# Hybrid RG-LRU and attention encoder block: four weight sums of group H on VectorE instead of in the transfers, and turned gate rows turned and stored at other ticks

## The chip, the cores and the metric

The kernel runs on one core of a Trainium2 chip. The time is device time in microseconds (us) of one execution. The kernel before takes 885.68 us, the median of three runs (883.79 to 886.96).

A core has five engines that run side by side, each with its own queue of instructions, worked off in order: TensorE (PE in the profile, with its weight loads as PEld), VectorE (DVE), ScalarE (ACT), GpSimd (POOL) and SyncE (SP). SP, POOL and ACT also issue transfers (DMA) between DRAM and the on-chip memory. A transfer can add what it brings to what already stands in the destination; here only POOL issues such transfers.

## The reference, cut to what matters

One layer, 256 tokens, width 2048, all in float32:

```python
xn = rms_norm(x, norm_pre_w)
u_lru, g_lru, q, k, v, g_attn, m_lru, m_attn = split(xn @ w_in)      # w_in is 2048 x 13312
h   = rg_lru forward + rg_lru backward of a width-4 convolution of u_lru
y_a = h * silu(g_lru)
y_b = windowed_gqa(rope(q), rope(k), v, sink) * silu(g_attn)
merged = sigmoid(m_lru) * (y_a @ w_proj_a) + sigmoid(m_attn) * (y_b @ w_proj_b)
out = x + rms_norm(merged @ w_out, norm_post_w)
```

The change is in how half of `g_attn` is made: columns 1024 to 2047 of that gate, which the kernel calls group H.

## The kernel before, in words

All the weights stream from DRAM through one list of steps (`START`, `MERGE`, `OUT`), some 190 of them, each with 128 x 2048 float32 numbers (1 MB) of weights in two halves. To keep float32 accuracy, every half `raw` is split in two: ScalarE casts it to a short form `wh` (L222), VectorE subtracts that from the original and gets the remainder `wl` (L224). TensorE then makes three products per block: `wh` with the two parts of the activations, and `wl` with the first part. So each step costs ScalarE two casts and VectorE two subtractions of 128x1024.

Six stretches of columns are not multiplied plainly but by a seven-product scheme (class `Seven`, groups L, H, M, N, A, O; the matmuls are on L435). Four quarter blocks of the weights, (0,0), (0,1), (1,0) and (1,1), make seven products m1 to m7, taken in the order m1, m2, m5, m3, m6, m7, m4. The weights of the products m1, m5, m6 and m4 are running sums in a cell `x`: it is loaded with quarter (0,0), then (0,1), (1,1) and (1,0) are added in turn. The cell `y` is loaded with (1,1) for m3, and (0,1) is added for m7. Each cell exists for two inner halves (0, 1) with two tiles each (a, b): `Hx0a`, `Hx0b`, `Hx1a`, `Hx1b`, and `Hy..` likewise. The first load of a cell is a plain transfer by SP (L197); each addition is an adding transfer by POOL (L195), 512 KB per tile. For the groups named in the table `ADDED`, some of these additions are made otherwise: m6 needs the quarter (1,1) that m3 has just put in `y`, so VectorE adds `y` to `x` (L227), right behind the subtraction that makes m3's `wl`. Before the change this is so for A, O and N.

An adding transfer must wait until the subtraction L224 of the step before has read the cell, and the cast of its own step must wait until it has landed.

The products of H give rows of tokens, where attention needs rows of channels. `silu_rows` handles the four results, named `hr200`, `hr210`, `hr211` and `hr201` in order of time: a VectorE combination (L797), a sigmoid (L824), a product (L825), then four transposes on TensorE into a PSUM bank pair `ht` (L831), a ScalarE copy out of it (L832) and a store of 256 KB to DRAM by SP (L839, `parksga<-hr`), from where the gate is fetched much later.

When all this stands in the queues is set at the build. Time is counted in ticks, one for a product step and two for a plain block. `at(tick, fn)` and `soon(fn, d)` put the instructions of `fn` into the queues when the list reaches that tick. `seconds` holds the ticks at which the second block of a pair begins; a turn is put at the first of them that lies more than two ticks ahead, since it takes one of the two PSUM pairs that plain blocks also use. The store is put five ticks behind the turn.

Almost all large tiles (`wh`, `wl`, the cells, `hr`, gates, parked rows) come from one pool of 45 buffers. Which buffer a new tile gets is decided at the build from the order in which old tiles are given up. A tile's first writer then waits for the last readers of the old one, and where the last reader is a store, for its landing. The raw weights have a ring of three buffers of their own, so SP's queue is in step with VectorE: a load of raw weights (L210) waits for the subtraction that frees its buffer, and what stands behind it in SP's queue waits too.

Of the kernel before, what the change touches and what calls it, by code (L numbers as in the profile page):

```python
# [64 lines left out]
LRU = (-4, 0, 0, 0, 0, 0, 0, 0)  # L65
QUADS = {"u": ("w_in", U0), "v": ("w_in", V0), "p": ("w_proj_a", 0),
         "b": ("w_proj_b", 0), "o": ("w_out", 0)}
ADDED = {'A': {'m3': 'm6', 'm2': 'm4'}, 'O': {'m3': 'm6'}, 'N': {'m3': 'm6'}}
PAIRS = {"g": GL0, "h": GA0, "w": U0, "k": K0, "q": Q0}
SEVENS = {"L": ("w_in", ML0 + 1024), "M": ("w_in", ML0), "N": ("w_in", MA0), "A": ("w_in", MA0 + 1536), "H": ("w_in", GA0 + 1024), "O": ("w_out", 0)}  # L70

# [39 lines left out]
def body(ctx, tc, x, x0, xT, wall, wlru, pvec, npost, ident_d, mask_d, rope_d, out):  # L111
# [9 lines left out]
    def unit(name, dt=F32, shape=(P, 4, S)):  # L121
        return units.tile(list(shape), dt, tag="u", name=name)
# [4 lines left out]
    def banks(name, shape=(P, 2, 2, S)):  # L127
        return psum.tile(list(shape), F32, tag="mm", name=name, bufs=2)

    def half_unit(name, tag, dt=F32, bufs=2):  # L130
        return small.tile([P, 2, S], dt, tag=tag, name=name, bufs=bufs)
# [20 lines left out]
    now = [0]  # L152

    def ticks(i=None):
        return sum(1 if p[0] == "part" else 2 for p in plan[:len(steps) if i is None else i])

    def at(hs, fn):
        assert hs >= now[0], (hs, now[0])
        due.setdefault(hs, []).append(fn)
# [9 lines left out]
    seconds, hs, n = [], 0, 0  # L169
# [7 lines left out]
    def soon(fn, d=1):  # L177
        at(now[0] + d, fn)
# [11 lines left out]
    def load(cell, p, add=False):  # L190

        w = wall[row[content(p)]]
        for h in range(2):
            if add:
                nc.gpsimd.dma_start(flat(cell[h]), w[:, h * 1024:(h + 1) * 1024], accum_op=ALU.add)  # L195
            else:
                nc.sync.dma_start(flat(cell[h]), w[:, h * 1024:(h + 1) * 1024])  # L197
# [14 lines left out]
    def split(q, c=0, w=1024, cast=nc.scalar.copy, only=None):  # L212
# [10 lines left out]
        if only != "h":  # L223
            nc.vector.tensor_tensor(ls, raw, hs.bitcast(F32), ALU.subtract)  # L224
            if plan[i][0] == "part" and plan[i][2] in ADDED.get(plan[i][1], ()):
                x = flat(groups[plan[i][1]].cells["x", plan[i][3]][h])
# [137 lines left out]
    def x_sum(name, s, q):  # L364
        t = unit(name, F32R, (P, 4, 2, P))
        nc.sync.dma_start(t.rearrange("p a b c -> p a (b c)").bitcast(F32), away[q][:, SUMS.index(s)])
        return t

    class Seven:
# [22 lines left out]
        def fetch(self, p, lead):  # L392
            m, q = p[2:]
            fresh = ("m1", "m3") if self.sums is None else ()
            if self.sums is None:
                if lead == 4 and m in fresh:
                    self.start(self.where(m), q)
                if lead == 4 and SEVEN[m][0][0] == "s" and self.name in "NA":
                    self.kept[m, q] = x_sum(f"{self.name}{m}{q}", SEVEN[m][0], q)
            if lead == 5 and m in ("m5", "m6", "m7", "m4")[self.sums is not None:] and m not in ADDED.get(self.name, {}).values():  # L400
                load(self.cell(m, q), p, True)
# [394 lines left out]
    def combine(to, ps, other, sign):  # L796
        nc.vector.scalar_tensor_tensor(to, ps, float(sign), other, ALU.mult, ALU.add if sign > 0 else ALU.subtract)  # L797
# [17 lines left out]
    def silu_rows(g):  # L815

        def done(t, c, ps, other, sign):
            u = unit(f"hr{g}{c}{t}")
            f, y = flat(u)[:, 0:512], u[:, 2:4].rearrange("p a (b s) -> p (a b) s", b=2)
            rt = rtok[:, t:t + 1]  # L820

            def sigmoid(src):
                sg = flat(half_unit(f"hs{c}{t}", "p"))
                nc.scalar.activation(sg, src, AF.Sigmoid, scale=rt)  # L824
                soon(lambda: nc.vector.scalar_tensor_tensor(f, src, rt, sg, ALU.mult, ALU.mult))  # L825
                at(min(b for b in seconds if b > now[0] + 2), turn)

            def turn():
                pt = banks(f"ht{c}{t}", (P, 4, P))
                for j in range(4):  # L830
                    nc.tensor.transpose(pt[:, j], f[:, j * P:(j + 1) * P], ident)  # L831
                nc.scalar.copy(y, pt)  # L832
                soon(store, 5)

            def store():
                key = "sga", g + c
                if key not in parked:
                    parked[key] = dram.tile([P, 1024], F32, name=f"parksga{g + c}")
                nc.sync.dma_start(parked[key].rearrange("p (j s) -> p j s", j=4)[:, :, t * P:(t + 1) * P], y)  # L839

            if other is None:
                sigmoid(ps)
            else:
                combine(f, ps, other, sign)
                soon(lambda: sigmoid(f))
        return done
# [317 lines left out]
    b, n = ticks(), ticks(len(plan))  # L1164
# [159 lines left out]
```

## Time and profile before

| | |
|---|---|
| median of three runs | 885.68 us (883.79 to 886.96) |
| the profiled execution's own time | 884.68 us |
| its span (first to last instruction) | 882.9 us |
| TensorE busy | 862.4 us |
| VectorE busy | 750.3 us |
| ScalarE busy | 657.3 us |
| transfers, mean over the span | 277 GB/s |
| the stretch of group H | 248 to 357 us |

The profile shows one execution. Times in its rows are us from the span's start; a row of the time line has start, duration, engine, line, operation, output<-inputs, shapes, count, and in square brackets how long the engine had stood idle before it and what ended that. A row of the waits has the sum, the count and the longest. Names stand without buffer numbers there: `wl` is any remainder tile, `hr` any of the four gate rows. TensorE is busy nearly all the time, so what counts is what makes it stand still, and not how busy the others are on average.

### The profile page before, as it was taken

The numbers are of one execution on the slowest core, as the hardware profiler recorded it, in microseconds if no ns is written. First come the engines' busy times: TensorE is split into PE (matmuls) and PEld (weight loads), VectorE is DVE, ScalarE is ACT, GpSimd is POOL, SyncE is SP. The second block draws the span as 40 slices with busy tenths as digits, with TensorE's granted clock in tenths as the row PEclk, the third lists the DMA queues.
The fourth block names the chain that finished last, engine by engine and source line by source line (L and its number), as shares of the span: only waits on it lengthen the run. The fifth ranks groups of instructions, "written<-read, shape, count | busy, mean of one in ns | idle before, by whom it ended". The sixth has DMA issues, their size and how long they took to land.

```text
span 882.9 us, 12249 instructions
## 1 busy us (share of the span) xinstructions
PE 862.4 (98%) x4378; PEld 733.9 (83%) x4378; DVE 750.3 (85%) x999; ACT 657.3 (74%) x939; POOL 73.0 (8%) x105
## 2 busy tenths in 40 slices
PE   9999999999999979999999999999999999999996
PEld 8888888888888868788888888778888888788885
DVE  6998999898898869797897887897669778998886
ACT  7689698969879868987976779996558545665654
POOL 0000001022011200112100020000000100000200
PEclk9999999999999999999999999999999999999999
DMA  9757699999999985999989998798999987988982
GB/s 328 275 191 250 196 315 290 278 298 250 306 255 350 260 206 195 293 270 295 280 270 328 305 288 301 251 324 334 272 327 370 298 325 215 309 311 316 266 205 95
DMA packets 68045, 244.77 MB, mean 277 GB/s; under 512 B 6416, under 2 KB 24592, under 8 KB 53264
## 3 DMA queue, kind: packets, MB, share of 16 engines
q1 hardware_dynamic: 52480, 198.37, 61.4%
q0 software_dynamic: 11520, 41.95, 25.1%
q10 hardware_dynamic: 3984, 3.67, 1.3%
q8 instruction: 34, 0.56, 0.2%
q14 instruction: 27, 0.22, 0.1%
HBM read 223.52 MB, written 20.45 MB: 276 GB/s over the span
## 4 chain that ended last, share of the span: by engine, by line
PE 81%; DMA 5%; DVE 5%; issue 4%; ACT 2%; SPq 1%; ACTq 1%; POOLq 0%; DVEq 0%
PE q L258 6%; PE gl L258 6%; PE u L258 5%; PE Lm L435 4%; PE Nm L435 4%; PE Hm L435 4%; PE Am L435 3%; PE ga L258 3%; PE q L256 3%; PE gl L256 3%; PE Om L435 3%; PE Mm L435 3%; PE pb__7297 L278 2%; PE pa__5741 L278 2%; PE pa__5992 L278 2%
## 5 line engine op out<-in xcount | busy, mean ns | idle before, releaser
L224 DVE TENSOR_TENSOR wl<-raw,wh 128x1024 fp32r<-128x1024 f32 (+1 forms) x240 | 285.2, 1201 | 53.1 <-ACT wh L222 38.6
L222 ACT CAST wh<-raw 128x1024 fp32r<-128x1024 f32 (+1 forms) x239 | 241.1, 1035 | 60.9 <-DMA raw<-wall_dram 31.1
L258 PE MATMUL gl<-xs,wh 128*128 128x512 f32 x256 | 64.8, 397 | 0.0
L258 PE MATMUL q<-xs,wh 128*128 128x512 f32 x256 | 63.9, 392 | 0.0
L258 PEld LDWEIGHTS gl<-xs,wh 128*128 128x128 f32 x256 | 48.1, 193 | 9.4
L258 PEld LDWEIGHTS q<-xs,wh 128*128 128x128 f32 x256 | 46.8, 188 | 9.0
L258 PE MATMUL u<-xs,wh 128*128 128x512 f32 x192 | 47.6, 391 | 0.0
L258 PEld LDWEIGHTS u<-xs,wh 128*128 128x128 f32 x192 | 35.1, 188 | 6.7
L256 PE MATMUL gl<-xs,wl 128*128 128x256 f32 x256 | 34.3, 285 | 5.1 <-DVE wl L224 5.1
L256 PEld LDWEIGHTS gl<-xs,wl 128*128 128x128 f32 x256 | 33.1, 191 | 7.0 <-DVE wl L224 5.7
L256 PEld LDWEIGHTS q<-xs,wl 128*128 128x128 f32 x256 | 33.0, 191 | 1.3
L256 PE MATMUL q<-xs,wl 128*128 128x256 f32 x256 | 33.5, 283 | 0.0
L258 PE MATMUL ga<-xs,wh 128*128 128x512 f32 x128 | 31.8, 391 | 0.0
L258 PEld LDWEIGHTS ga<-xs,wh 128*128 128x128 f32 x128 | 23.3, 189 | 4.3
L256 PEld LDWEIGHTS u<-xs,wl 128*128 128x128 f32 x192 | 24.7, 191 | 0.9
L256 PE MATMUL u<-xs,wl 128*128 128x256 f32 x192 | 25.1, 283 | 0.0
L686 DVE SCALAR_TENSOR_TENSOR uu<-upad,pv,uu 128x256 f32<-128x256 f32 x48 | 23.1, 482 | 1.7
L943 DVE CUSTOM_DVE_ANT_0 p<-sc,table,pv 128x256 f32<-128x256 f32 x32 | 16.0, 538 | 4.5 <-PE sc L233 4.5
L709 ACT ACTIVATE gr<-gate,pv 128x256 f32<-128x256 f32 x32 | 15.2, 475 | 5.9 <-DMA parkya<-sg 5.1
L231 PE MATMUL gate<-ul,lwh 128*128 128x256 f32 x64 | 18.2, 284 | 0.5 <-ACT gi L710 0.5
L949 ACT ACTIVATE p<-p,nm 128x256 f32<-128x256 f32 x32 | 16.0, 501 | 3.1 <-DVE nm L944 3.1
L233 PE MATMUL gate<-ul,lwl 128*128 128x256 f32 x64 | 18.1, 283 | 0.0
(567 smaller groups left out, 2230.9 us busy)
## 6 DMA issues: line engine op xcount, KB each, us to landing
raw<-wall_dram SPq DMA_DIRECT2D x115, 1024.0 KB, 7.8
lraw<-wlru_dram SPq DMA_DIRECT2D x8, 512.0 KB, 7.5
away<-xx SPq DMA_DIRECT2D x8, 512.0 KB, 8.3
Nm<-away SPq DMA_DIRECT2D x8, 512.0 KB, 9.5
turn<-pt SPq DMA_DIRECT2D x32, 128.0 KB, 6.0
pl<-turn SPq DMA_DIRECT2D x8, 512.0 KB, 6.8
Am<-away SPq DMA_DIRECT2D x8, 512.0 KB, 7.5
raw<-wall_dram SPq DMA_DIRECT2D x8, 256.0 KB, 5.1
```

The source lines that it names most:

```text
L222: cast(hs, raw)
L224: nc.vector.tensor_tensor(ls, raw, hs.bitcast(F32), ALU.subtract)
L231: nc.tensor.matmul(ps, wh, xh, start=start, stop=False, skip_group_check=more)
L233: nc.tensor.matmul(ps, wl, xh, start=False, stop=stop, skip_group_check=more)
L256: nc.tensor.matmul(ps[:, 1], wl[:, sl], a[:, 0], start=False, stop=False)
L258: nc.tensor.matmul(ps, wh[:, sl], a, start=k == 0, stop=k == KT - 1)
L278: nc.tensor.matmul(got[t], a[:, i], (wl if low else wh)[:, sl], start=k + low + i == 0, stop=low == 1 and k == KT - 1)
L435: nc.tensor.matmul(self.ps[b], a[i], (wl if low else wh)[:, sl], start=fresh and j + low + i == 0, stop=last and j + low == 2, skip_group_ ...
L686: nc.vector.scalar_tensor_tensor(u, up[:, j, tap:tap + S], cw[:, tap:tap + 1], u, ALU.mult, ALU.add)
L709: nc.scalar.activation(v["gr"][:, 2 * d + j], ps[:, 0], AF.Sigmoid, bias=pv[:, PV_BR + b:PV_BR + b + 1])
L943: nc.vector.tensor_tensor_reduce(p[:, t], sc[:, t], table["mask"][:, t], rtok_sc[:, t:t + 1], sk, ALU.add, ALU.max, m[:, t:t + 1])
L949: nc.scalar.activation(p[:, t], p[:, t], AF.Exp, bias=nm[:, t:t + 1], accum_out=dn[:, t:t + 1])
```

## The change

Three constants change. Group H joins the table `ADDED` for m6: POOL no longer issues the four adding transfers of m6, and VectorE makes four additions of 128x1024 behind the subtractions of m3. The turn is put at the first second block more than four ticks ahead, not two. The store is put two ticks behind the turn, not five.

```diff
-ADDED = {'A': {'m3': 'm6', 'm2': 'm4'}, 'O': {'m3': 'm6'}, 'N': {'m3': 'm6'}}
+ADDED = {'A': {'m3': 'm6', 'm2': 'm4'}, 'O': {'m3': 'm6'}, 'N': {'m3': 'm6'}, 'H': {'m3': 'm6'}}
...
-                at(min(b for b in seconds if b > now[0] + 2), turn)
+                at(min(b for b in seconds if b > now[0] + 4), turn)
...
                 nc.scalar.copy(y, pt)
-                soon(store, 5)
+                soon(store, 2)
```

The order of the built programs shows what this does to the queues. First VectorE at steps 59 and 60, the two halves of m3 of group H (`wl59`, `wl60`); the rows of before:

```order
L224 TENSOR_TENSOR wl59_0_2903<-Hy0a_2818,wh59_0_2902 128x1024
L617 TENSOR_TENSOR sg8_2528<-gl10_2770,sg8_2528 128x512
L613 TENSOR_TENSOR sg8_2528<-sg8_2528,rbc_93 128x512
L224 TENSOR_TENSOR wl59_1_2913<-Hy0b_2819,wh59_1_2912 128x1024
L729 SCALAR_TENSOR_TENSOR gr8_2553<-a8_2706,gi8_2554 128x256
L730 SCALAR_TENSOR_TENSOR gr8_2553<-a8_2706,gi8_2554 128x256
L224 TENSOR_TENSOR wl60_0_2942<-Hy1a_2850,wh60_0_2941 128x1024
```

And of after, the same place:

```order
L224 TENSOR_TENSOR wl59_0_2901<-Hy0a_2818,wh59_0_2900 128x1024
L227 TENSOR_TENSOR Hx0a_2352<-Hx0a_2352,Hy0a_2818 128x1024
L617 TENSOR_TENSOR sg8_2528<-gl10_2770,sg8_2528 128x512
L613 TENSOR_TENSOR sg8_2528<-sg8_2528,rbc_93 128x512
L224 TENSOR_TENSOR wl59_1_2911<-Hy0b_2819,wh59_1_2910 128x1024
L227 TENSOR_TENSOR Hx0b_2353<-Hx0b_2353,Hy0b_2819 128x1024
L729 SCALAR_TENSOR_TENSOR gr8_2553<-a8_2706,gi8_2554 128x256
L730 SCALAR_TENSOR_TENSOR gr8_2553<-a8_2706,gi8_2554 128x256
L224 TENSOR_TENSOR wl60_0_2941<-Hy1a_2850,wh60_0_2940 128x1024
L227 TENSOR_TENSOR Hx1a_2439<-Hx1a_2439,Hy1a_2850 128x1024
```

Each subtraction has an addition behind it; the fourth follows three rows further on.

Second, who waits for the store of the first gate row, `hr200`. It signals its landing on the semaphore DMAHW5 in both programs. VectorE of before, steps 62 to 64, with what each instruction waits for:

```order
L224 TENSOR_TENSOR wl62_1_3048<-Hx0b_2353,wh62_1_3047 128x1024 [waits DVE_49,DMASW5_49,PE_49,Activation_49]
L714 TENSOR_TENSOR gi10_2965<-gi10_2965,uu10_2762 128x512 x2
L224 TENSOR_TENSOR wl63_0_3073<-raw63_3029,wh63_0_3072 128x1024 [waits DMAHW2_49,DVE_49,Activation_49]
L224 TENSOR_TENSOR wl63_1_3095<-raw63_3029,wh63_1_3094 128x1024 [waits DMAHW5_49,PE_49,Activation_49]
L224 TENSOR_TENSOR wl64_0_3126<-Hx1a_2439,wh64_0_3125 128x1024 [waits DMASW6_49,PE_49,Activation_49]
```

VectorE of after:

```order
L224 TENSOR_TENSOR wl62_1_3048<-Hx0b_2353,wh62_1_3047 128x1024 [waits DVE_49,PE_49,Activation_49]
L714 TENSOR_TENSOR gi10_2965<-gi10_2965,uu10_2762 128x512 x2
L224 TENSOR_TENSOR wl63_0_3073<-raw63_3029,wh63_0_3072 128x1024 [waits DVE_49,DMAHW2_49,PE_49,Activation_49]
L224 TENSOR_TENSOR wl63_1_3095<-raw63_3029,wh63_1_3094 128x1024 [waits DVE_49,PE_49,Activation_49]
L224 TENSOR_TENSOR wl64_0_3128<-Hx1a_2439,wh64_0_3127 128x1024 [waits DVE_49,PE_49,Activation_49]
```

The second remainder of step 63, `wl63_1`, no longer waits for DMAHW5: it has another buffer. ScalarE of after, at the cast of step 65:

```order
L750 ACTIVATE gr10_2964<-a10_3118 128x1024 [waits Activation_49]
L682 ACTIVATE uu12_3150<-upad12_2709,pv_76 128x256 [waits Pool_49]
L222 CAST wh65_0_3154<-raw65_3114 128x1024 [waits DMAHW5_49,DMAHW4_49]
L682 ACTIVATE uu12_3150<-upad12_2709,pv_76 128x256
L222 CAST wh65_1_3182<-raw65_3114 128x1024 [waits DVE_49,PE_49]
```

The buffer of `hr200` now goes to `wh65_0`, so this cast waits for DMAHW5; before, it waited for its raw weights and TensorE alone.

Third, SP's queue between steps 80 and 85, of before:

```order
L210 DMA raw80_3724<-wall_dram 128x2048
L863 DMA parkya2_3781<-sg8_2528 128x1024
L839 DMA parksga3_3595<-hr211_3359 512x1x128
L839 DMA parksga2_3206<-hr201_3540 512x1x128
L210 DMA raw82_3811<-wall_dram 128x2048
L197 DMA My0a_3813<-wall_dram 128x1024
L197 DMA My0b_3814<-wall_dram 128x1024
L197 DMA My1a_3844<-wall_dram 128x1024
L197 DMA My1b_3845<-wall_dram 128x1024
L210 DMA raw85_3933<-wall_dram 128x2048
L1129 DMA table_3425<-mask_dram 128x512
L863 DMA parkq0_4010<-q0f_3512 128x1024
```

Of after:

```order
L839 DMA parksga3_3512<-hr211_3359 512x1x128
L210 DMA raw80_3719<-wall_dram 128x2048
L863 DMA parkya2_3776<-sg8_2528 128x1024
L210 DMA raw82_3804<-wall_dram 128x2048
L197 DMA My0a_3806<-wall_dram 128x1024
L197 DMA My0b_3807<-wall_dram 128x1024
L197 DMA My1a_3837<-wall_dram 128x1024
L197 DMA My1b_3838<-wall_dram 128x1024
L839 DMA parksga2_3121<-hr201_3542 512x1x128
L210 DMA raw85_3933<-wall_dram 128x2048
L1129 DMA table_3425<-mask_dram 128x512
L863 DMA parkq0_4010<-q0f_3514 128x1024
```

The store of `hr211` comes two transfers earlier, that of `hr201` five later, in front of raw 85, the mask table and the parking of q. VectorE's `wl83_0` takes the buffer of `hr201` and waits for that store; `wl84_0` waits for the parking of q in both programs. Higher up in the queue the store of `hr210` has moved ahead of the raw loads of steps 75 and 76. On TensorE and ScalarE one thing alone moves: the four transposes of `hr201` and the copy behind them. Before, they stand directly behind those of `hr211`, at the start of step 75; after, at the start of step 80, where on ScalarE the copy comes ahead of the unpacking of q (L913). The first turn, the second and the third keep their places, and so does the store of `hr200` in SP's queue. From step 92 on, the tiles that reuse a buffer follow the same kinds of readers at the same distances as before.

## The prediction

> **What bounds the kernel now.** I read the page's busy times first, then TensorE's waits, then the chain that ended last, then the time line where that chain leaves TensorE.
>
> ```profile
> PE 862.4 (98%) x4378; PEld 733.9 (83%) x4378; DVE 750.3 (85%) x999; ACT 657.3 (74%) x939; POOL 73.0 (8%) x105
> PE gl L256 <- DVE wl L224: 5.1, 2, 3.9
> 303.69 12.96 DMA parksga<-hr
> ```
>
> TensorE is busy 98% of the span, so there is little to win: some 20 us of standing still in all (882.9 less 862.4). The longest wait inside is for a remainder `wl`: 5.1 us in two pieces, at gate step 63 and 65. The chain passes there through the store of a gate row of group H, 12.96 us from issue to landing. The time line tells why:
>
> ```profile
> 303.69 0.52 SPq L839 DMA_DIRECT2D parksga<-hr  x1
> 305.52 1.22 DVE L224 TENSOR_TENSOR wl<-raw,wh 128x1024 fp32r<-128x1024 f32 x1
> 313.02 1.11 PE L256 MATMUL gl<-xs,wl 128*128 128x256 f32 x8
> 313.51 1.03 ACT L222 CAST wh<-raw 128x1024 fp32r<-128x1024 f32 x1
> 316.77 1.23 DVE L224 TENSOR_TENSOR wl<-raw,wh 128x1024 fp32r<-128x1024 f32 x1 [10.02 <-DMA parksga<-hr]
> 318.05 1.41 PE L256 MATMUL gl<-xs,wl 128*128 128x256 f32 x8 [3.92 <-DVE wl L224]
> 319.26 3.43 PE L258 MATMUL gl<-xs,wh 128*128 128x512 f32 x8
> 325.25 1.98 PE L258 MATMUL gl<-xs,wh 128*128 128x512 f32 x8
> 329.33 1.22 PE L256 MATMUL gl<-xs,wl 128*128 128x256 f32 x8 [1.15 <-DVE wl L224]
> 318.00:322.50 4.50, 4.45 (x16) 3.75 (x17) 4.43 (x6) 0.00 (x0) 1.38 (x2) 0.62 0.81 244
> ```
>
> `wl63_1` was given the buffer of `hr200`. VectorE, whose queue is in order, stands 10.02 us until the store has landed at 316.65. TensorE stands 3.92 us for it, from 314.13. The last row is a window: busy times of the engines, then the granted clock, 0.62. So the stall is paid twice: eight matmuls of 256 columns take 1.41 us where the eight before took 1.11, and eight of 512 take 3.43 where the same form takes 1.98, together 1.75 us. VectorE, late, costs another 1.15 us at step 65.
>
> **Term 1, the first store's buffer: 5.9 us gained.** In the new order `wl63_1` has another buffer and waits only for work long done, so the 10.02 us go, with 3.92 of TensorE's idle time and 1.75 of low clock: 5.67. What is late next is VectorE itself, since it gets four additions.
>
> ```profile
> L227 DVE TENSOR_TENSOR Nx0a<-Nx0a,Ny0a x1: 1219/1219/1219, 497.7 to 497.7; 128x1024 f32<-128x1024 f32 x1
> 297.11 1.22 DVE L224 TENSOR_TENSOR wl<-Hy1b,wh 128x1024 fp32r<-128x1024 f32 x1 [0.71 <-ACT wh L222]
> 301.76 0.41 PEld L435 LDWEIGHTS Hm<-wl,xx 128*128 128x128 f32 x2
> ```
>
> The same addition in group N takes 1.22 us, so four cost 4.88. They stand where VectorE has no idle time but 0.71, so everything behind them comes 4.17 later. Does TensorE feel it? `wl60_1`, with three additions ahead of it, ends at 298.33 + 3.66 - 0.71 = 301.28, and TensorE loads it at 301.76: 0.5 to spare, the tightest place. `wl63_1` would start at 306.74 + 4.17 = 310.9 and end at 312.1, against 314.13 where TensorE wants it. So the additions cost TensorE nothing, at best 0, at worst 4.17 if that spare half microsecond is gone throughout. Behind it VectorE is 10.02 - 4.17 = 5.85 earlier than before and TensorE 5.67, so the gap at step 65 shrinks by 0.2 and not by 1.15 (the two ends). The term is 3.92 + 1.75 + 0.2 = 5.9.
>
> The new owner of that buffer is `wh65_0`, cast by ScalarE. With the landing as measured the cast starts at 316.65, not 313.51, and ends at 317.7. TensorE wants it at the start of step 65, which moves to 325.25 - 5.67 = 319.6: 1.9 to spare. Behind the cast ScalarE goes on to work that waited for VectorE in any case. Price 0, other end below under the rivals.
>
> **Term 2, the four adding transfers of m6: 0.**
>
> ```profile
> 273.89 0.86 POOL L195 DMA_DIRECT2D Hx0a<-wall_dram  x1 [18.48 <-DVE wl L224]
> 291.44 0.86 POOL L195 DMA_DIRECT2D Hy0a<-wall_dram  x1 [4.27 <-DVE wl L224]
> 326.00 1.04 ACT L222 CAST wh<-Hy0a 128x1024 fp32r<-128x1024 f32 x1
> q0 software_dynamic: 11520, 41.95, 25.1%
> q1 hardware_dynamic: 52480, 198.37, 61.4%
> ```
>
> They were issued from 273.89 on and nobody waited for them. They leave some transfer time: the adding queue takes 0.251 x 882.9 / 41.95 = 5.3 us of all engines per MB, so 11 us for 2.1 MB, just ahead of the store of `hr200`, which can only land sooner. I take no gain from it. POOL's next four, for m7, now wait for the additions, up to 4 us later, but the first of them is issued at 291.44 and cast at 326.00: hidden.
>
> **Term 3, the fourth turn: 1.67 gained.**
>
> ```profile
> 367.86 4.62 DVE L224 TENSOR_TENSOR wl<-raw,wh 128x1024 fp32r<-128x1024 f32 x4
> 368.63 0.60 PE L831 MATMUL ht<-ident,hr 128*128 128x128 f32 x4
> 370.27 0.57 ACT L832 COPY hr<-ht 128x512 f32<-128x512 f32 x1
> 370.90 0.66 PE L831 MATMUL ht<-ident,hr 128*128 128x128 f32 x4 [1.67 <-ACT hr L832]
> ```
>
> Two turns follow each other, and the second needs the PSUM pair that the first one's copy has yet to free. With the second turn five steps later TensorE goes from 369.23 into step 75. Its first remainder is the first of the four VectorE makes from 367.86 on, done at 369.1, and needed 1.84 us into the step. So all 1.67 are gained; the other end is 0, if the same wait comes at step 80 for the other pair. I take 1.67: there one turn stands alone, as at the first two turns, where no wait shows.
>
> **Term 4, the stores moved in SP's queue: 0 and 1.2 lost.**
>
> ```profile
> 346.71 2.80 SPq L210 DMA_DIRECT2D raw<-wall_dram  x2
> 350.52 0.53 SPq L839 DMA_DIRECT2D parksga<-hr  x1
> 364.12 1.05 ACT L222 CAST wh<-raw 128x1024 fp32r<-128x1024 f32 x1
> raw<-wall_dram SPq DMA_DIRECT2D x115, 1024.0 KB, 7.8
> ```
>
> The second store waits for its copy until 350.5, and now two raw loads stand behind it, the first 4.4 us later than before, at 351.1. With the median 7.8 it lands at 358.9, well ahead of its cast at 364.12. The third store moves up by two places and waits for a copy done before the next ring buffer is free. Both cost 0. The fourth now stands ahead of raw 85, the mask and the parking of q:
>
> ```profile
> 390.77 1.68 ACT L913 COPY q0f<-q0r 32x256 f32<-32x256 f32 x4
> 390.96 0.33 SPq L197 DMA_DIRECT2D My1b<-wall_dram  x1
> 399.83 1.22 DVE L224 TENSOR_TENSOR wl<-My0a,wh 128x1024 fp32r<-128x1024 f32 x1
> 408.65 0.61 PE L435 MATMUL Mm<-wl,xx 128*128 128x512 f32 x2
> 410.98 1.23 DVE L224 TENSOR_TENSOR wl<-My1a,wh 128x1024 fp32r<-128x1024 f32 x1 [5.62 <-DMA parkq<-q0f]
> 412.26 0.72 PE L435 MATMUL Mm<-wl,xx 128*128 128x512 f32 x2 [0.73 <-DVE wl L224]
> My1b<-wall_dram SPq DMA_DIRECT2D x1, 512.0 KB, 7.6
> parkq<-q0f SPq DMA_DIRECT2D x1, 512.0 KB, 18.0
> raw<-wall_dram SPq DMA_DIRECT2D x1, 1024.0 KB, 22.2
> DMA to landing us min/median/max: 8.2/9.1/13.0
> ```
>
> Here transfers are slow: the parking of q takes 18.0 us, VectorE waits 5.62 for it and TensorE 0.73. The fourth copy delays the unpacking of q by 1.2 (0.60 of transposes, 0.59 of copy), and the 256 KB store stands in front: at 0.614 x 882.9 / 198.37 = 2.7 us per MB another 0.7. If the queue is long, only the 0.7 counts; if not, 1.9. I take 1.2, nearer the first since 18.0, against 7.6 for the transfer issued 2 us earlier, shows a long queue. Ends: 0.73 gained, if the wait goes, and the case below. VectorE's `wl83_0` waits for the store itself: issued about 392.3 (390.77 + 1.2 and the issue, an estimate), with the 8.2 to 13.0 us of the four stores before, it lands at 400.5 to 405.3, so VectorE stands up to 5.5 us behind 399.83, but TensorE wants the remainder at 408.65. No price up to 15.1 us.
>
> The Trainium skill, DMA: Bandwidth & Descriptors, "Queues, rings and completion order", says that a DMA engine works off one queue's ring in order and alternates with other queues. By that rule the store lands right behind My1b, the loss is the 0.7 alone and the sum 877.8 in place of 878.3. The trace agrees as far as it goes: My1b at 398.5 and the parking at 410.9 landed in their order of issue.
>
> **Sum.** 5.9 + 1.67 - 1.2 = 6.4 against the profiled execution's 884.68 (span 882.9): 878.3. The median shown, 885.68, is 1.0 above that execution; I forecast halfway, 878.8, and from 876.5 to 882.5 if this case holds.
>
> **Rivals.** *Every gap here goes* (term 1 with all of 1.15, the 0.73 too): 884.68 - 3.92 - 1.75 - 1.15 - 1.67 - 0.73 = 875.5. For it: fewer transfers. Against: VectorE is as late to step 65 as before. 0.12.
>
> *The wait only moves to ScalarE.* If the store of `hr200` lands later than 318.6, 14.9 us after its issue, `wh65_0` holds up TensorE. At the 22.2 us of the slowest row it lands at 325.9, the cast ends 326.9, the gap is 7.3 and the clock 1.75: 9.1 in place of 6.8, with 0.5 from the rest 886.4. Against it: 12.96 in a fuller queue. With it I count that the additions eat the spare 0.5 and several small waits give back 4 us: 882.5 to 887. 0.13.
>
> *Slower: the fourth store's buffer.* At `wl83_0` the same trap can close again. If the store takes 22.2 us, as the raw load issued beside it did, it lands at 414.5, `wl83_0` is ready at 415.7, TensorE stands 7.1 us, loses 1.75 of clock, and some 2 more (an estimate) while VectorE catches up with three more remainders: 10.8 less the 0.73, against 7.6 gained: 887.2. It makes the change slower from 19.7 us on. For it: 18.0 and 22.2 in this stretch. Against: those stood behind 1.25 MB and more that this store precedes. 0.09.
>
> That the change does nothing is excluded: the order shows both moves.
>
> **Numbers.** My case 0.66. The range 875 to 886.5 takes in the first two cases and most of the third and leaves out some 0.14. Faster by over 0.3% (2.7 us, about what a measurement can tell) 0.78, within 0.13, slower 0.09.
>
> **What would show it.** No VectorE wait for `parksga` near 310; the clock at 1.00 there; a ScalarE wait for `parksga` of at most 3 us ahead of a cast; no wait of TensorE's turns for a copy; a wait for the parking of q that is still there, at 400 (6 earlier), with a TensorE wait of 1 to 2 us. I am wrong if TensorE waits at group H's m3 or m6 for VectorE, at step 65 for ScalarE, or at group M's m3 for more than 5 us.

## The result: no measurable change

The changed kernel takes 885.06 us (median of 12 runs, 882.59 to 890.3), the kernel before, beside it, 884.93 us (12 runs, 882.89 to 888.53). The ratio is 1.000, with a 95% interval of 0.9985 to 1.0016. I had forecast 878.8 us.

The profiled execution of after took 890.3 us (span 888.5). That is the longest of its 12, so the two traces are compared stretch by stretch. The starts of the same matmuls in both, after less before:

| before at us | 150.0 | 210.0 | 305.1 | 340.0 | 372.6 | 402.1 | 425.0 | 874.1 |
|---|---|---|---|---|---|---|---|---|
| after later by us | 0.75 | 6.23 | 6.04 | 1.34 | -0.99 | 3.33 | 5.53 | 5.63 |

The 6 us by which after is late at 305 arise ahead of anything the change touches, near 196 (last section). From 305 to 373, in group H, after wins 7.03 us. From 373 to 425, in group M, it loses 6.52 of them again. Everything behind is the same. So the win that I forecast came, and was given back within 50 us.

In group H the profile of after shows this (time line of ScalarE, VectorE and TensorE, then a window):

```profile
315.38 1.22 DVE L224 TENSOR_TENSOR wl<-raw,wh 128x1024 fp32r<-128x1024 f32 x1
324.68 1.05 ACT L222 CAST wh<-raw 128x1024 fp32r<-128x1024 f32 x1 [5.03 <-DMA parksga<-hr]
329.62 1.22 PE L256 MATMUL gl<-xs,wl 128*128 128x256 f32 x8 [0.77 <-DVE wl L224]
331.47 1.23 DVE L224 TENSOR_TENSOR wl<-Hy0a,wh 128x1024 fp32r<-128x1024 f32 x1 [1.90 <-ACT wh L222]
333.43 0.73 PE L435 MATMUL Hm<-wh,xx 128*128 128x512 f32 x2 [0.75 <-ACT Hu L447]
318.00:322.50 4.50, 4.50 (x29) 4.05 (x28) 4.43 (x6) 1.62 (x3) 1.46 (x2) 1.00 1.06 281
parksga<-hr SPq DMA_DIRECT2D x1, 256.0 KB, 14.9
```

VectorE no longer waits for the first store, TensorE's 3.92 us and the low clock are gone. But the store takes 14.9 us to land, where it took 12.96, and ScalarE now stands 5.03 us for it at step 65. Behind that VectorE stands 0.46 and 1.90 for ScalarE, and TensorE 0.77 and 0.75. (In run 11, where ScalarE doesn't stand for the store, 0.28 of the 0.77 is left, and the 0.75 is gone.) In group M:

```profile
380.08 2.00 ACT L222 CAST wh<-raw 128x1024 fp32r<-128x1024 f32 x2 [3.29 <-DMA raw<-wall_dram]
381.16 1.23 DVE L224 TENSOR_TENSOR wl<-raw,wh 128x1024 fp32r<-128x1024 f32 x1 [3.20 <-ACT wh L222]
390.44 1.22 DVE L224 TENSOR_TENSOR wl<-Mx0b,wh 128x1024 fp32r<-128x1024 f32 x1
391.71 0.73 PE L435 MATMUL Mm<-wl,xx 128*128 128x512 f32 x2 [2.07 <-DVE wl L224]
392.28 0.66 PE L831 MATMUL ht<-ident,hr 128*128 128x128 f32 x4
392.63 3.66 PE L258 MATMUL gl<-xs,wh 128*128 128x512 f32 x8
392.00:397.00 5.00, 5.00 (x22) 4.11 (x22) 5.00 (x6) 4.91 (x9) 0.89 (x1) 0.66 0.73 139
404.65 1.22 DVE L224 TENSOR_TENSOR wl<-My0a,wh 128x1024 fp32r<-128x1024 f32 x1 [2.35 <-DMA parksga<-hr]
416.51 1.22 DVE L224 TENSOR_TENSOR wl<-My1a,wh 128x1024 fp32r<-128x1024 f32 x1 [6.85 <-DMA parkq<-q0f]
417.79 0.73 PE L435 MATMUL Mm<-wl,xx 128*128 128x512 f32 x2 [2.93 <-DVE wl L224]
parkq<-q0f SPq DMA_DIRECT2D x1, 512.0 KB, 19.7
```

At step 79 (m5 of M) TensorE stands 2.07 us for `wl79_1`, where before showed no wait, and the clock falls to half (0.66 over 392 to 397; eight matmuls of 512 take 3.66 us). VectorE works from 381.16 to 402.3 without a pause, so it can't catch up. It starts there when ScalarE has cast raw weights that have just landed: those of the load one place ahead of raw 80 in SP's raw loads, issued at 372.31 in after and at 370.24 in before.

```profile
raw<-wall_dram SPq DMA_DIRECT2D x1, 1024.0 KB, 7.7
raw<-wall_dram SPq DMA_DIRECT2D x1, 1024.0 KB, 5.6
378.76 1.23 DVE L224 TENSOR_TENSOR wl<-raw,wh 128x1024 fp32r<-128x1024 f32 x1 [1.62 <-ACT wh L222]
```

The first row is this load in after, the second in before, the third is before's row for 381.16 above. In all ten profiles that have a wait at step 79, that of after and nine of the runs below, the wait ends 11.7 us after this load has landed. In before TensorE came there 14.47 us after the landing, so it had 2.76 to spare. The 2.07 can be added up from three shifts of after against before, counted from the same matmul near 340: TensorE comes to step 79 1.96 us sooner; the load is issued 0.74 later, 7.8 us behind a VectorE subtraction (364.53, `wl` of Mx1a) that is late by as much; and it takes 2.13 more to land. 1.96 + 0.74 + 2.13 - 2.76 = 2.07.

Behind this the parking of q takes 19.7 us (18.0 before), and TensorE stands 2.93 for it (0.73 before).

### The profile page after: what moved, and what is told of

The parts are those of the page before. It is cut to its first block, busy times and chain, and to the rows that moved or that the text cites. A ratio compares the mean times of both kernels' runs of the same rounds, so it can differ in the third digit from the quotient of the medians.

```text
span 888.5 us, 12251 instructions
## 1 busy us (share of the span) xinstructions
PE 866.8 (98%) x4378; PEld 736.8 (83%) x4378; DVE 754.5 (85%) x1003; ACT 657.7 (74%) x939; POOL 69.5 (8%) x101
## 4 chain that ended last, share of the span: by engine, by line
PE 75%; DMA 9%; DVE 7%; issue 5%; ACT 3%; ACTq 1%; SPq 0%; POOLq 0%; DVEq 0%
PE gl L258 5%; PE u L258 5%; PE q L258 4%; PE Lm L435 4%; PE Hm L435 4%; PE Am L435 3%; DVE wl L224 3%; PE Om L435 3%; PE ga L258 3%; PE u_ps L581 3%; DMA raw<-wall_dram 3%; PE pb__7297 L278 2%; PE pa__5741 L278 2%; PE o__7556 L278 2%; PE pa__5992 L278 2%
## 5 line engine op out<-in xcount | busy, mean ns | idle before, releaser
L224 DVE TENSOR_TENSOR wl<-raw,wh 128x1024 fp32r<-128x1024 f32 (+1 forms) x240 | 284.7, 1200 | 48.0 <-ACT wh L222 40.9
L231 PE MATMUL gate<-ul,lwh 128*128 128x256 f32 x64 | 18.7, 293 | 2.7 <-ACT gi L710 2.7
L232 PE MATMUL gate<-ul,lwh 128*128 128x256 f32 x64 | 18.6, 291 | 0.0
```

The costliest lines, as they stand in the source:

```text
L231: nc.tensor.matmul(ps, wh, xh, start=start, stop=False, skip_group_check=more)
L232: nc.tensor.matmul(ps, wh, xl, start=False, stop=False, skip_group_check=more)
```

## The experiments

First the table of all of them. "Won" and "lost" come from each kernel's one profile, by the same reckoning as above: the shift against the trace of before from 305.1 to 372.6, and from there to 425.0. A minus under "lost" is a further gain. Where the fourth turn stays at step 75 (but for runs 5 and 12, where it has its own bank), both traces have a wait there, so it is not among what is won; in run 3 it is 2.36 with low clock, which the 3.1 has paid for.

| run | median us (runs) | ratio to before, 95% interval | won in H | lost in M |
|---|---|---|---|---|
| changed kernel | 885.06 (12) | 1.000, 0.9985 to 1.0016 | 7.0 | 6.5 |
| 1 additions alone | 881.48 (12) | 0.9958, 0.9936 to 0.998 | 6.8 | -0.4 |
| 2 turn and stores alone | 888.04 (12) | 1.0023, 1.0005 to 1.0041 | 1.9 | 2.9 |
| 3 fourth turn at step 75 | 879.95 (6) | 0.993, 0.9909 to 0.9951 | 3.1 | -1.0 |
| 4 stores issued by ScalarE | 894.64 (6) | 1.0093, 1.007 to 1.0116 | 1.3 | 8.8 |
| 5 as 3, turn in its own bank | 880.52 (6) | 0.9934, 0.991 to 0.9957 | 8.7 | 0.9 |
| 6 as 3, fourth store late | 886.96 (12) | 1.0009, 0.9985 to 1.0033 | 6.9 | 5.9 |
| 7 fourth store behind the parking | 891.45 (7) | 1.0062, 1.0034 to 1.0091 | 7.1 | 11.6 |
| 8 changed kernel again | 883.11 (10) | 0.9956, 0.9931 to 0.9981 | 7.3 | 4.0 |
| 9 changed kernel, third time | 885.16 (12) | 0.9989, 0.9967 to 1.0011 | 8.5 | 6.8 |
| 10 as 3, again | 882.01 (12) | 0.9952, 0.993 to 0.9973 | 6.9 | 1.5 |
| 11 first store sooner | 882.25 (12) | 0.996, 0.9941 to 0.998 | 9.0 | 5.4 |
| 12 as 5, first store sooner | 877.76 (7) | 0.9897, 0.9868 to 0.9925 | 8.1 | 1.3 |
| 13 second store back | 885.34 (12) | 0.9996, 0.9975 to 1.0017 | 6.6 | 7.2 |
| 14 parking of q first | 883.89 (12) | 0.998, 0.9959 to 1.0002 | 7.2 | 2.9 |

Runs 1 to 4 shared a chip and the runs of the kernel before, and so did 5 to 8, 9 to 12, and 13 and 14. The changed kernel was timed against the kernel before three times, with 1.000, 0.9956 and 0.9989: between no change and 0.4% faster.

**1. The additions alone.**

```diff
-ADDED = {..., 'N': {'m3': 'm6'}}
+ADDED = {..., 'N': {'m3': 'm6'}, 'H': {'m3': 'm6'}}
```

> Group H in ADDED alone; turns and stores as before. The changed kernel's trace shows 7.0 us won between 310 and 370 and 6.5 lost between 390 and 420. Theory 1 (the loss comes from the moved stores: the second in front of raw 75 and 76, the fourth in front of the parking of q): here the win of 5.3 for the first store's buffer stays, the 1.67 of the fourth turn doesn't, no loss follows: 879 to 881, no low clock near 392. Theory 2 (the loss follows whatever TensorE wins in H, since ScalarE now waits about 5 us for the first store at step 65 and VectorE stays 2 us late to step 80): 884 to 886, a TensorE wait near 390 for a remainder. Theory 3 (the additions themselves cost): above 886.

881.48 us, 0.42% faster. The additions alone already send the buffer of the first row to `wh65_0`; the win in H is whole, and next to nothing is lost in M. Theory 3 falls: the four additions cost no measurable time. Theory 1 is the nearer, but Theory 2, which supposed that ScalarE waits 5 us for the store, isn't out: in this profile it waits 2.15.

**2. The turn and the stores alone**, without the additions: the other two lines of the change.

> Turn and store constants alone; no additions, so wl63_1 waits for the first store as before. Theory 1: the 10 us wait of VectorE and the 3.9 of TensorE stay, the 1.67 of the fourth turn goes, the losses near 392 (4.1 with the clock) and at the parking of q (2.2) come: 888 to 890. Theory 2: no loss but at most the parking of q: 883 to 886, no low clock near 392.

888.04 us, 0.23% slower. The first wait is there as before, and worse (`[4.38 <-DVE wl L224]` in place of 3.92):

```profile
319.07 1.23 PE L256 MATMUL gl<-xs,wl 128*128 128x256 f32 x4 [4.38 <-DVE wl L224]
389.77 0.73 PE L435 MATMUL Mm<-wl,xx 128*128 128x512 f32 x2 [0.64 <-DVE wl L224]
411.38 0.74 PE L435 MATMUL Mm<-wl,xx 128*128 128x512 f32 x2 [0.73 <-DVE wl L224]
413.84 0.73 PE L435 MATMUL Mm<-wl,xx 128*128 128x512 f32 x2 [0.79 <-DVE wl L224]
```

The time is Theory 1's, the mechanism only half: the wait near 390 is 0.64 and has no low clock. In the sum above the 0.74 is missing here, and the raw load lands in 6.8 us, 0.9 less than in after. So the moved turn and stores alone don't make the 2.07.

**3. The fourth turn at step 75**, all else as changed.

```diff
-                at(min(b for b in seconds if b > now[0] + 4), turn)
+                at(min(b for b in seconds if b > now[0] + (4 if (c, t) != (0, 1) else 2)), turn)
```

> The changed kernel, but the fourth turn stands where it stood before, at step 75, with its store two ticks behind it, ahead of raw 80. The second store is still in front of raw 75 and 76. If the fourth store in front of the parking of q is what costs (2.2 us), the parking lands sooner, the wait there falls to 1 us or less, and 1.67 comes back at the turn: about even with the changed kernel, and the wait near 391 stays. If the second store in front of the raw loads is what costs, the wait near 391 (2.07 and low clock) stays too. If the fourth turn is the cause of the wait near 391, it goes: 881.

879.95 us, 0.7% faster. Both waits in M are gone, so it is the fourth turn and its store that the changed kernel pays for:

```profile
318.74 1.05 ACT L222 CAST wh<-raw 128x1024 fp32r<-128x1024 f32 x1 [4.49 <-DMA parksga<-hr]
367.03 1.11 PE L831 MATMUL ht<-ident,hr 128*128 128x128 f32 x4 [2.36 <-ACT hr L832]
386.59 0.62 PE L435 MATMUL Mm<-wl,xx 128*128 128x512 f32 x2
387.95 0.62 PE L435 MATMUL Mm<-wl,xx 128*128 128x512 f32 x2
400.00:425.00 25.00, 25.00 (x139) 21.58 (x138) 19.08 (x22) 22.13 (x32) 4.37 (x5) 1.00 1.04 293
```

The turn's wait is back, 2.36 with low clock behind it, and yet it costs less than what it saves: TensorE comes to step 79 that much later and finds its remainders there.

**4. The stores issued by ScalarE.**

```diff
-                nc.sync.dma_start(parked[key].rearrange(...), y)
+                nc.scalar.dma_start(parked[key].rearrange(...), y)
```

> The changed kernel, but the four stores are issued by ScalarE, so SP's queue doesn't stand for the copies, and the buffers of the four rows go elsewhere (the first to a cast at group w's step 64 behind it, lwh12; the fourth to wh84_0). Theory 1: the win in H stays (7.0), raw 75 and 76 are issued at 346 to 350 again, the wait near 391 goes, the parking costs 1 to 2: 879 to 881. Theory 2: TensorE still waits near 391 for VectorE: 884 to 886.

894.64 us, 0.93% slower, which neither theory had. The buffers moved on: that of the first row to `lwh12`, that of the fourth to `wh84_0`, and ScalarE, which feeds VectorE, waits for both stores.

```profile
328.38 1.04 ACT L143 CAST lwh<-lraw 128x1024 fp32r<-128x1024 f32 x1 [7.87 <-DMA parksga<-hr]
332.37 2.08 PE L435 MATMUL Hm<-wh,xx 128*128 128x512 f32 x4 [4.63 <-ACT Hu L447]
418.06 1.04 ACT L222 CAST wh<-My1a 128x1024 fp32r<-128x1024 f32 x1 [13.87 <-DMA parksga<-hr]
419.16 2.07 PE L435 MATMUL Mm<-wh,xx 128*128 128x512 f32 x4 [6.96 <-ACT wh L222]
```

It doesn't tell Theory 1 from 2, but shows what a buffer still being stored costs.

**5. As 3, with a PSUM bank for the fourth turn alone**, so that it needn't wait for the third one's copy.

```diff
-                pt = banks(f"ht{c}{t}", (P, 4, P))
+                pt = (bank if (c, t) == (0, 1) else banks)(f"ht{c}{t}", (P, 4, P))
```

> The third experiment (fourth turn at step 75, 879.95 us), but the fourth turn has a single PSUM bank of its own and needn't wait for the third turn's copy. Theory A (TensorE is bounded here by VectorE's remainders, which come no sooner than their raw weights land; what the turn's wait takes TensorE would stand anyway some 20 us later): the turn's wait of 2.36 and its low clock (1.7) go, but a wait of 2 to 3 us for a remainder of M's m5 appears near 388: 878.5 to 882. Theory B (the turn's wait is a loss of its own): no new wait, 876 to 878.3.

880.52 us; the ratio 0.9934 is that of run 3, 0.993. The turn's wait is gone, and two others have come:

```profile
363.48 1.03 PE L831 MATMUL ht<-ident,hr 128*128 128x128 f32 x8
384.55 0.74 PE L435 MATMUL Mm<-wl,xx 128*128 128x512 f32 x2 [1.17 <-DVE wl L224]
388.89 1.22 PE L256 MATMUL gl<-xs,wl 128*128 128x256 f32 x8 [0.80 <-DVE wl L224]
```

1.17 + 0.80 = 1.97, about what the wait of 1.67 to 2.36 had been. That is Theory A, at a smaller size than expected and without low clock: behind the turn TensorE is bounded by VectorE, and VectorE by the landing of the raw load, here too 11.7 us ahead of the first wait's end. The second wait is not the turn's alone: run 1, where the turn still waits, has 0.83 at that place, while runs 3, 6 and 10 have 0.34 or less. And this profile is of the fastest of the six executions, 877.08 us; what waits the median one has is not known.

**6. As 3, with the fourth store late**, seven ticks behind the turn, at its place in the changed kernel.

```diff
-                soon(store, 2)
+                soon(store, 2 if (c, t) != (0, 1) else 7)
```

> The third experiment (fourth turn at step 75), but the fourth store is put seven ticks behind it, between My1b and raw 85, ahead of the mask and the parking of q, where the changed kernel has it. The buffer goes to wh83_1, a cast. Theory C (the store's place is what costs the changed kernel its win): the parking of q lands 1 to 2 later, VectorE waits for it longer than 4.5, or ScalarE waits for the store at wh83_1: 882 to 885. Theory A (the turn's place is): 879.5 to 881.

886.96 us. Against run 3 everything won is lost, though the turn is where it was: Theory C, and by more than it said.

```profile
401.21 1.04 ACT L222 CAST wh<-My0b 128x1024 fp32r<-128x1024 f32 x1 [8.42 <-DMA parksga<-hr]
403.05 0.58 PE L231 MATMUL gate<-ul,lwh 128*128 128x256 f32 x1 [4.89 <-ACT gi L710]
```

Here the late store's buffer goes to a cast, and ScalarE stands 8.42 us; in the changed kernel it goes to `wl83_0`, where VectorE's 2.35 hurt nobody. So a late store costs by who gets its buffer, and this run doesn't measure the changed kernel's own store.

**7. The changed kernel with the fourth store behind the parking of q.**

```diff
-                soon(store, 2)
+                soon(store, 2 if (c, t) != (0, 1) else 8)
```

> The changed kernel (fourth turn at step 80), but the fourth store is put eight ticks behind the turn: behind the parking of q and one more raw load, so that nothing of step 80 to 85 stands behind it; its buffer goes to th14, used much later. Theory A (with no wait at step 75 TensorE runs ahead of VectorE and stands near 390, low clock and all): the wait of about 2 near 391 stays, 882 to 884.5. Theory C (the store's place): 878.5 to 880.5.

891.45 us, worse than either theory had it. The wait near 387 is there, 2.07, as Theory A said, though without its low clock; but now q's buffer goes to the cast `wh84_1`, the row's to `th14`, and ScalarE waits for both:

```profile
387.11 0.73 PE L435 MATMUL Mm<-wl,xx 128*128 128x512 f32 x2 [2.07 <-DVE wl L224]
388.03 2.09 PE L258 MATMUL gl<-xs,wh 128*128 128x512 f32 x8
409.86 1.04 ACT L222 CAST wh<-My1b 128x1024 fp32r<-128x1024 f32 x1 [7.74 <-DMA parkq<-q0f]
421.12 1.71 ACT L721 ACTIVATE th<-gr,cpos 128x256 f32<-128x256 f32 x4 [6.35 <-DMA parksga<-hr]
423.81 1.72 PE L435 MATMUL Mm<-wh,xx 128*128 128x512 f32 x4 [3.88 <-ACT wh L222]
```

**8 and 9. The changed kernel again**, twice.

> The changed kernel a second time, for a second profile. If the losses in group M belong to the change, a wait of TensorE for a remainder between 385 and 395 and one for the parking of q between 405 and 420 are here too, together over 3 us with the low clock, while the wait of 2.72 near 199, ahead of anything changed, is another size: 882.5 to 887.

> The changed kernel a third time, on one chip with the three below, since its two medians stand at 1.000 and 0.9956 of the kernel before. If the turn at step 75 and at step 80 are worth the same and only the late store costs, it lies 0.2 to 0.5% above the next run: 882 to 885; a wait near 387 to 391 of about 2 with low clock is in the profile again.

883.11 and 885.16 us. The wait at step 79 is in both profiles, and of the same size, with low clock behind it (2.06 in run 8). The wait for the parking of q is in run 9 but not in run 8, where VectorE waits 2.69 for it and TensorE 0.30.

```profile
386.05 0.73 PE L435 MATMUL Mm<-wl,xx 128*128 128x512 f32 x2 [2.08 <-DVE wl L224]
412.13 0.73 PE L435 MATMUL Mm<-wl,xx 128*128 128x512 f32 x2 [2.92 <-DVE wl L224]
```

So the first belongs to the change, the second comes and goes from one execution to the next.

**10. Run 3 again**, on the chip of run 9.

> The third experiment again (fourth turn at step 75, its store at step 77). If the fourth turn and store are what the changed kernel loses, 879 to 881.5, and the ratio to the run before it below 0.9975. If the difference between them was that of two chips, both lie within 0.2%.

882.01 us, half a microsecond above what was expected, but 3.15 below the changed kernel beside it (0.9964 of it by the medians). The difference isn't one of chips. Its profile has no wait at step 79, but one of 1.85, with no low clock, at the remainder that waits for the parking of q.

**11. The changed kernel with the first store one place sooner** in SP's queue, ahead of raw 65.

```diff
-                soon(store, 2)
+                store() if (c, t) == (0, 0) else soon(store, 2)
```

> The changed kernel, but the first store is put in SP's queue one place sooner, ahead of raw 65, the megabyte issued before it. Theory D (the 5 us that ScalarE waits for the first store at step 65 make it and VectorE late up to group M, and half of the wait near 390 is due to that): the wait at step 65 falls from 5 to 2 or less, the waits of 0.77 and 0.76 near 324 and 328 go, the one near 388 falls from 2.06 to about 1.2 with no low clock: 879.5 to 881.5. Rival (ScalarE's wait there is covered, and raw 65, late by 5 us, takes its place): as the changed kernel or slower, 883 to 887.

882.25 us, 2.9 below the changed kernel on the same chip.

```profile
parksga<-hr SPq DMA_DIRECT2D x1, 256.0 KB, 6.6
316.71 1.05 ACT L222 CAST wh<-raw 128x1024 fp32r<-128x1024 f32 x1 [0.87 <-DMA raw<-wall_dram]
384.53 0.74 PE L435 MATMUL Mm<-wl,xx 128*128 128x512 f32 x2 [0.83 <-DVE wl L224]
385.46 2.10 PE L258 MATMUL gl<-xs,wh 128*128 128x512 f32 x8
```

The store lands in 6.6 us in place of 14.9. ScalarE doesn't wait for it, raw 65 is 0.87 late, TensorE's waits behind step 65 shrink from 0.77 and 0.75 to 0.28 and none, and that at step 79, 60 us later, falls from 2.07 to 0.83 with no low clock. Those are the steps of Theory D, but the last one isn't its doing alone. In the sum above VectorE is no longer late, which takes off 0.74; the raw load lands in 7.0 us, which takes off another 0.70; and TensorE comes 0.20 sooner. The time lies between Theory D's range and the rival's; the parking of q has its wait in this profile too (3.00, with low clock).

**12. Run 5 with the first store sooner**, both edits.

> The fifth experiment (fourth turn at step 75 in a bank of its own, 880.5) and the first store ahead of raw 65. Theory D: the small waits at 324 and 328 stay away in every execution and the one near 385 is 1.2 or less: 876.5 to 879. Rival (raw 65 late): 880 to 884.

877.76 us, ratio 0.9897 (0.9868 to 0.9925): the fastest here, 1% faster than the kernel before and 0.8% than the changed one. The median lies in Theory D's range, but the profile, of the slowest of the seven executions (882.27 us), doesn't go by it. The wait at step 79 is 1.56, without low clock, where 1.2 was the most. And raw 65, now behind the store, lands so late that ScalarE waits 3.07 us for it and TensorE 0.77 near 328, as the rival had it. TensorE doesn't wait for the parking of q.

**13. The changed kernel with the second store back** at five ticks.

```diff
-                soon(store, 2)
+                soon(store, 5 if (c, t) == (1, 0) else 2)
```

> The changed kernel, but the second store is put five ticks behind its turn, as before, so raw 75 and 76 stand ahead of it in SP's queue. Theory E (the wait near 390 comes from raw weights that SP issues late, behind the second store): raw 75 and 76 are issued some 4 us sooner, the wait of 2.07 near 388 falls below 1 and its low clock goes: 880.5 to 882.5. Theory D (it comes from ScalarE's wait at step 65 and from TensorE being ahead): the wait stays at about 2, 883.5 to 886.

885.34 us, no gain; its profile also has the wait for the parking of q, 3.90 and low clock. Against TensorE's own position raw 75 and 76 are issued 4.4 and 2.6 us sooner than in after (344.7 and 347.2, with TensorE 3.3 ahead of before; 353.8 and 354.5, with TensorE 1.3 behind), and the wait at step 79 is 1.70 in place of 2.07. Theory E holds for a small part at most; the load ahead of raw 80, which lands in 7.1 us and not in 7.7, covers the difference.

**14. The changed kernel with the parking of q ahead** of the fourth store, raw 85 and the mask.

```diff
-QAWAY = 10
+QAWAY = 7
```

> The changed kernel, but the parking of q is put seven ticks behind its block, not ten, so it stands ahead of the fourth store, raw 85 and the mask; the buffer of q goes to gr14 (written by ScalarE), that of the fourth row to wh84_0 (a cast). If what stands ahead of the parking (1.5 MB) is what makes VectorE wait near 415, the parking lands in 10 us and not in 17 to 20, that wait and TensorE's 2.9 go, and the rest stays: 882 to 883.5. Rival (the waits only change their place: ScalarE now waits for the parking at gr14 or for the fourth store at wh84_0): 885 to 890.

883.89 us, 0.4 above what was expected.

```profile
390.24 0.73 PE L435 MATMUL Mm<-wl,xx 128*128 128x512 f32 x2 [2.07 <-DVE wl L224]
432.23 0.73 PE L435 MATMUL Mm<-wl,xx 128*128 128x512 f32 x2 [0.92 <-DVE wl L224]
parkq<-q0f SPq DMA_DIRECT2D x1, 512.0 KB, 7.5
```

The parking lands in 7.5 us, not 19.7, and TensorE's 2.93 fall away, so it was what stands ahead of it in the queue. The fourth row's buffer now goes to a cast, and ScalarE waits 3.31 for that store. The loss up to 425 falls from 6.5 to 2.9 in the trace, though 1.6 more follow behind it. In the time the gain over the kernel before is too small to be told from none.

## Why the prediction was wrong

Two steps failed: that the new owner of the first store's buffer has price 0 (Term 1), and that all of the fourth turn's 1.67 are gained (Term 3). Each looked at the next operand and no further, and what they missed came together at step 79, with a raw load that took 2.1 us longer to land than in the trace of before.

**Term 1, the first store's buffer, 5.9 gained.** The mechanism was right: with VectorE's wait went TensorE's 3.92 and the low clock. Won by 340 are 6.04 - 1.34 = 4.70. Where ScalarE waits only some 2 us at step 65 (2.0 to 2.2, runs 1, 5, 6 and 10), it is 6.8 to 6.9, all of 3.92 + 1.75 + 1.15. The sentence that failed is the one on the new owner of the buffer: "Behind the cast ScalarE goes on to work that waited for VectorE in any case. Price 0, other end below under the rivals." I had put the landing as measured, 12.96; in the eleven profiles that have the additions and this store at its old place it takes 11.9 to 15.3, and ScalarE waits 2.0 to 5.5. In after, with 5 us of it, VectorE is still 0.74 late at 364, against 0.05 at most where ScalarE waits some 2, and the raw load behind that is late by as much. Run 11 takes ScalarE's wait away: by 340 it has won 6.64, and it is 2.9 us faster than run 9 in the medians, though 0.70 of what it gains at step 79 in the trace is the raw load's sooner landing. My second rival, the wait that moves to ScalarE, is what happened, and its range, 882.5 to 887, holds the result. That is in part luck: it had TensorE stand for ScalarE at step 65 itself, which only run 13 shows, with 0.52, and it knew nothing of group M, where most was given back. I had given it 0.13, because I asked only whether TensorE would wait at step 65.

**Term 2, the four adding transfers of m6, 0.** Right for what was counted: run 1 has no cost of the additions. Wrong in the aside that the first store "can only land sooner" with them gone: it lands later in seven of those eleven profiles. The four adding transfers for m7 now wait for VectorE's additions, and the last of them is issued 0.5 us ahead of the store, where it was 4.0; that they delay it was not tried apart.

**Term 3, the fourth turn, 1.67 gained.** At 373 the gain is there: 1.34 + 0.99 = 2.33, the 1.67 and 0.66 of transposes now made later. "So all 1.67 are gained" failed some 20 us further on. I looked at step 75's own remainders, and not at step 79, where before had 2.76 to spare between the landing of the raw load and TensorE's coming. VectorE's lateness and the longer landing, 0.74 + 2.13, used that up, and the 1.96 by which TensorE came sooner became a wait. Where the turn keeps its wait (runs 1, 3, 6 and 10) there is none at step 79. Run 5 shows it from the other side: with the turn's wait gone by other means, 1.17 comes up at step 79 and 0.80 soon behind.

**Term 4, the stores in SP's queue, 0 and 1.2 lost.** That the raw loads behind the second store cost nothing held (run 13). The fourth store was mis-sized: 2.2 us are lost at the parking of q in two of three profiles of the changed kernel, none in the third, against 1.2 forecast. That transfers ahead of the parking make it, and not the copy, run 14 shows. The Trainium skill's rule that I had set against my figure (DMA: Bandwidth & Descriptors, "Queues, rings and completion order": a DMA engine works off one queue's ring in order) agrees with runs 11 and 14, where what was put ahead landed in 6.6 and 7.5 us in place of 14.9 and 19.7; the loss of 0.7 that I had worked out by it was too small all the same. The third rival, `wl83_0` waiting for the fourth store itself, was weighed rightly: VectorE waits 2.35 there, and TensorE not.

**The sum.** Forecast for this stretch was a gain of 6.4; the trace has 7.03 - 6.52 = 0.5. The wait at step 79 with its low clock and the turn's own 0.36 make up 2.07 + 1.70 + 0.36 of the 6.5, the parking 2.2. The wait at step 79 stood in none of my terms nor on the list of places that would prove me wrong. The list's bound on ScalarE's wait, 3 us, was passed, by 2.

Left open is why the raw load ahead of raw 80 takes longer: 5.6 us in the one trace of before, 5.8 in run 4, 6.8 in run 2 and 7.0 to 8.5 in all the others. No run holds it fixed, and whether before's other executions have 5.6 is not known. Left open is also how the 3.15 us between runs 9 and 10 divide between the fourth turn and the fourth store. Runs 6 and 7 move one of them alone, but each gives buffers to other owners, whose waits are larger than what was to be measured.

## What to carry to other kernels

When a buffer whose store is under way gets a new owner, price the wait on the engine that now has it, and follow that engine's lateness to the next place where it or the one it feeds has no idle time, however far. The time that an engine wins is kept only if its feeders are ahead at the next such place: find there when the operand is ready, what it waits for in turn (here a raw load), and when it is wanted, and subtract. Before a store is moved to another tick or engine, try its place in the queue: one place, ahead of a 1 MB load, more than halved its landing and was worth 0.3%; the load behind it can then be the late one, as run 12's profile shows.

## What the runs showed of the hardware

TensorE's clock falls to half after gaps far shorter than the one of 3.92 us in the first profile. Leaving out starts and ends of kernels, the 16 profiles hold seven gaps of 3.8 us and more, all followed by half clock; of 15 gaps between 1.8 and 3.1 us 11 are, and of ten between 1.45 and 1.75 none. The shortest is 1.81, while four are not: 2.93 of after at 417.79, 2.92 of run 9, 2.07 of run 7 (rows above: eight matmuls of 512 take 2.09 behind it, 3.66 in after) and 1.85 of run 10. The half clock lasts 3.41 us or twice that in the clock's records, about 1.7 us of loss for each 3.41 in which TensorE works. The Trainium skill, TensorE: Matmul & The Clock Gate, "HAM oscillation", gives as the rule that TensorE shouldn't idle for more than about 3.4 us; here that is too generous by almost half. The same page says, in "The HAM clock gate", that the window is 3413 ns and free-running, and both fit the records: the length is that of a window, the 187.73 us at full clock between the two stretches at half in the record of after are 55 of them, and whether a gap of 2 us counts changes from one execution to the next.

A small wait can make much of the scatter. Near 196 us, in group L, the recurrence's gates need a PSUM bank that ScalarE has to empty:

```profile
195.41 0.39 PE L231 MATMUL gate<-ul,lwh 128*128 128x256 f32 x1 [0.53 <-ACT gi L710]
198.90 0.58 PE L231 MATMUL gate<-ul,lwh 128*128 128x256 f32 x1 [2.72 <-ACT gi L710]
200.00:205.00 5.00, 5.00 (x17) 4.27 (x17) 3.77 (x4) 4.37 (x9) 1.11 (x2) 0.51 1.05 288
```

The first row is of before, the others of after. Over the 16 profiles the wait lies between less than 0.4 and 3.07 us, and in five of them half clock follows. That alone can set two executions of one kernel 6 us apart: from 150 to 210 the trace of after loses 5.5 us against before, that of run 8, the same kernel, gains 0.6. No experiment here touched it.
